# A state-space loop in another order: the turn-back split between two engines, input products dealt over three steps, half of a norm taken earlier

## The chip, the cores and the metric

The kernel runs on one core of a Trainium2 chip. The core has five engines that run on their own queues, each in order: TensorE (PE, matrix products into PSUM), VectorE (DVE, elementwise work and scans), ScalarE (ACT, functions and copies), GpSimd (POOL, here some elementwise work), SyncE (SP, here the queue that issues nearly all DMAs). They wait for each other through semaphores. The metric is the device time of the whole program in microseconds, the median of several runs. The profiled execution is one more run, with a trace of every instruction.

## The reference, cut to what matters

A trunk of two layers on one sequence of 512 positions and 1024 features. Each layer is a half-step SwiGLU, a token mixer and another half-step SwiGLU, all with an RMSNorm before and after. The mixer of layer 0 is an S5 state-space layer, that of layer 1 a convolution module. The change lies in layer 0:

```python
x = x + 0.5 * rmsnorm(swiglu(rmsnorm(x, g_pre)), g_post)
h = rmsnorm(x, norm_pre)
u = h @ w_in                               # 64 groups of 16
bu = einsum(u, B_bar)                      # complex, 64 states a group
st[t] = a_bar * st[t-1] + bu[t]            # complex scan over the positions
y = gelu(Re(C st) + d_skip * u)
z = y * sigmoid(y @ w_glu + b_glu)
h = z @ w_out
x = x + rmsnorm(h, norm_post)
```

All products are in float32. The kernel makes them of float32r halves: a matrix is split into a high part (rounded) and a low part (the rest), and three matmuls, high x high, high x low and low x high, make one product.

## The kernel before, in words

The six sub-layers run one after another (L1378): ffn, s5, ffn, ffn, conv, ffn. x stays in SBUF, features on the partitions, as eight pieces of 128 x 512. Weights come as units of 128 x 1024: `want(n)` (L87) splits unit n on ACT (L94, high part) and DVE (L98, low part) and issues the load (L83, on SP) of the unit three further on. `mm3` (L108) issues the three matmuls (L110 to L112). Buffers are pools whose tiles are handed out in program order: 39 pages of 128 x 1024, five `tmp`, eight PSUM banks, two `acc` and two `y` tiles. There is no planner here: the instructions stand on each engine in the order in which the Python code issues them.

**The seam.** `proj` (L251) ends a sub-layer. Its tail (L366) goes over 16 pieces (half A of the positions for k = 0 to 7, then half B) in steps s: `scaled` (DVE L350), `added` (DVE L354; ACT L173 makes the high half of the next input, L177 the square), `split_lo` (DVE L186, of the piece two steps back), `x_plus` (DVE L182, which adds the squares into acc2), and `entry_step`, 12 matmuls that start the next sub-layer's first four units with that piece. A small list `side` puts the three DVE steps of half B's output norm between them, one a step. The sum over features of acc2 is `stat`, a matmul with ones (L117); `rsqrt_steps` (L120) is one ACT function (L123) and three DVE operations (L125 to L127). Before, `entry_norm` (L241) takes this entry norm over all 512 positions at once, on PE after the first product of the next sub-layer.

**The state-space layer.** `s5` (L833) has eight units j of w_in. `win(j)` is unit j's product, 24 matmuls; 0 to 3 are done in the seam. `stack(j)` scales the bank with the norm (DVE L855), and a DMA writes it to DRAM; `unstack(j)` reads it back in another layout. Then nine steps s of a loop (L980) work on tile s of eight, several stages at once:

- `inputs(s)`: PE, 8 products (L867) into two banks (real and imaginary).
- `turn(s)`: four DVE products of banks with tables (L880, L881, L883, L884), a POOL sum (L882) and a DVE difference (L885).
- `scan(s)`: two DVE scans (L892), with coefficients made by `decay` (ACT L873, POOL L874).
- `back(s-1)`, the turn-back of the scanned tile: POOL memsets (L904), a POOL product (L905) and three DVE products (L906 to L908).
- `outputs(s-1)`: PE, 20 products (L917, L920) into a bank; `gelu(s-1)` on ACT (L925); `y_out`, `y_in`: a DMA to DRAM and, a step later, back in the old layout.
- `parts(s-3)`: the high and low halves of y, on ACT (L940) and DVE (L941).
- `glu_step(s-3)`: PE, 12 matmuls of the gate product with piece s-3, which need both halves.

The order inside a step is partly written out (inputs, for s = 0 and 1 a whole win(6 + s), back, the DMAs) and partly given by the string `S5_ORDER` (L25), one letter for each part: k stack, t turn, w want, p parts, d decay, o outputs, c scan, g glu_step, l gelu. So PE has inputs(s), outputs(s-1), glu_step(s-3) in that order, and DVE has back(s-1), stack, turn(s), the weight split, parts(s-3), scan(s).

Of the kernel before, what the change touches and what calls it, by code (L numbers as in the profile page):

```python
# [9 lines left out]
AF = mybir.ActivationFunctionType  # L10
# [3 lines left out]
NK = 8  # L14
# [7 lines left out]

C_TAPS = (31, 31, None, None, None, None, None, 23)
NL = 2
S5_ORDER = "ktwpdocgl"  # L25
S5_WANT = (8, 9, 10, 11, 11, 11, 11, 11, 11)
BUD_D = (3, 8, 18, 18, 18, 18)
FFN_AHEAD = 4
# [7 lines left out]
def trunk(ctx: ExitStack, tc: tile.TileContext, h, plan):  # L36
# [15 lines left out]
    def page(dt=F32R):  # L52
        return pages.tile([P, 2, T], dt, tag="pg", name=nm("pg"))
# [7 lines left out]
    def psum():  # L61
        return psp.tile([P, T], F32, tag="ps", name=nm("ps"))
# [24 lines left out]
    def want(n):  # L87
        while ptr["split"] <= min(n, NU - 1):
            u = ptr["split"]
            w_dma(u)  # L90
            r = raws.pop(u)
            hi, lo = page(), page()
            hv, lv = hi.rearrange("p a b -> p (a b)"), lo.rearrange("p a b -> p (a b)")
            ACT.copy(hv, r)  # L94
            if lo_engine[0] is None:
                late.append((lv, r, hv))
            else:
                lo_engine[0].tensor_tensor(lv, r, hv.bitcast(F32), op=ALU.subtract)  # L98
            halves[u] = tuple(v.rearrange("p (k m) -> p k m", m=P) for v in (hv, lv))
            ptr["split"] += 1  # L100
            w_dma(u + 3)
# [28 lines left out]
    def rsqrt(ps, y):  # L130
        for f in rsqrt_steps(ps, y):
            f()
# [4 lines left out]
    def y_tile():  # L137
        return statp.tile([P, T], F32, tag="y", name=nm("y"))
# [51 lines left out]
    def entry_step(k, cs, xn, u0, ps4, outs=range(4)):  # L190
        for j in outs:
            mm3(ps4[j][:, cs], u0 + j, k, xn[k][:, 0, cs], xn[k][:, 1, cs], k == 0, k == NK - 1)
# [55 lines left out]
            e["acc"] = stat_tile()  # L248
            DVE.tensor_scalar(e["acc"], ps, EPS_SUM, EPS_SUM / P, op0=ALU.add, op1=ALU.mult)

    def proj(u0, nk, rhs, post, nl, pre, xn, bias=None, lead=None, carried=None, defer=True):  # L251

        acc = stat_tile() if carried is None else carried
        acc2 = stat_tile()
# [106 lines left out]
            else:  # L361
                (nc.sync, nc.scalar)[k % 2].dma_start(out=h["out"][:, k, cs], in_=x[:, k, cs])

        side, sqs = [], {}
        at = (2, 5, 5, 6) if pre is None else (4, 4, 4, 5)
        for s in range(len(todo) + 2):  # L366
            if s < len(todo):
                if s == NK:
                    while side:
                        side.pop(0)()  # L370
                scaled(*todo[s])
            if side:
                side.pop(0)()
            if 1 <= s <= len(todo):
                added(*todo[s - 1])
            if pre is not None and s == at[0]:
                sq = square(NK - 1, pb, B)
            if s == at[1]:
                plus(sq, B)
                if pre is None:  # L380
                    copy(NK - 1, pb, B)
            if pre is not None and s == at[2]:
                sb = stat(acc[:, B])
            if pre is not None and s == at[3]:
                copy(NK - 1, pb, B)
            if s >= 2 and pre is not None:
                cs, k = todo[s - 2]
                split_lo(k, cs, xn, pre)
                if s == 2:
                    want_late()  # L390
                if not defer:
                    x_plus(sqs.pop((cs.start, k)), cs, acc2)
                entry_step(k, cs, xn, un, ps4)
            if pre is None and s == at[0]:
                sq = square(NK - 1, pb, B)
            if pre is None and s == at[2]:
                sb = stat(acc[:, B])
            if s == at[3]:
                side = rsqrt_steps(sb, y[:, B], carried is None)
        if pre is not None and defer:  # L400
            want(un + 4)
            for k in range(NK):
                x_plus(x_square(k, FULL, acc2), FULL, acc2)
        return {"xn": xn, "ps": ps4, "acc2": acc2, "u": un} if pre is not None else None

    def ffn(e, post, pre, defer=True):
        u0, xn = e["u"], e["xn"]
        g = []

        def evac(m, pa, pb):  # L410
            a = tmp()
            DVE.tensor_tensor(a, pa, e["y"], op=ALU.mult)  # L412
            ACT.activation(a, a, AF.Silu)  # L413
            DVE.tensor_tensor(a, pb, a, op=ALU.mult)  # L414
            t = page()
            ACT.copy(t[:, 0, :], a)  # L416
            DVE.tensor_tensor(t[:, 1, :], a, t[:, 0, :].bitcast(F32), op=ALU.subtract)  # L417
            g.append(t)

        pend = None  # L420
        want(u0 + 6)
        for m in range(2, NF):
            pa, pb = psum(), psum()
            for j, ps in enumerate((pa, pb)):
                want(u0 + 2 * m + j)
                for k in range(NK):
                    mm3(ps, u0 + 2 * m + j, k, xn[k][:, 0, :], xn[k][:, 1, :], k == 0, k == NK - 1)
                    if m == 2 and j == 0 and k == 4:
                        entry_norm(e, True)
                    if k == 3:  # L430
                        n = 2 * m - 4 + j
                        tick("D", PREP_FIRST[n] if n < len(PREP_FIRST) else PREP_UP)
            if FFN_AHEAD and m > 2:
                want(u0 + 2 * m + FFN_AHEAD)
            if m == 2:
                ACT.preload_act_table(AF.Silu)
                evac(0, e["ps"][0], e["ps"][1])
                evac(1, e["ps"][2], e["ps"][3])
            else:
                evac(*pend)  # L440
            pend = m, pa, pb
            want(u0 + 2 * m + 2)
        evac(*pend)
        return proj(u0 + 2 * NF, NF, g, post, 1, pre, g[:NK], carried=e["acc"], defer=defer)

# [385 lines left out]
    def s5(e, post, pre):  # L833
# [62 lines left out]
        def back(i):  # L896


            X, Y = wk.pop(i)
            c, s = (tabs[i][2][:, r, :, :n] for r in range(2))  # L900
            S = page(F32).rearrange("p r (q c) -> p r q c", q=4)
            st[i] = S, X
            for v in (S, X):
                POOL.memset(v[:, :, :, 0:1], 0.0)  # L904
            POOL.tensor_tensor(S[:, 0, :, 1:], Y[:, 0, :, :n], c, op=M)  # L905
            DVE.scalar_tensor_tensor(X[:, 0, :, 1:], Y[:, 1, :, :n], -1.0, s, op0=M, op1=M)  # L906
            DVE.tensor_tensor(S[:, 1, :, 1:], Y[:, 0, :, :n], s, op=M)  # L907
            DVE.tensor_tensor(X[:, 1, :, 1:], Y[:, 1, :, :n], c, op=M)  # L908
# [32 lines left out]
                DVE.tensor_tensor(t[:, 1, :], yf[i], t[:, 0, :].bitcast(F32), op=D)  # L941

        banks = {j: e["ps"][j] for j in range(4)}
        cf = {}

        def win(j, norm=False):
            want(u0 + j)
            banks[j] = psum()
            for k in range(NK):
                mm3(banks[j], u0 + j, k, xn[k][:, 0, :], xn[k][:, 1, :], k == 0, k == NK - 1)  # L950
                if norm and k == 0:
                    entry_norm(e)

        g0 = u0 + 8

# [8 lines left out]
        load(0, (0, 3, 2))  # L964
        load(1, (0, 3, 2))
        load(0, (1,))
        want(u0 + 5)
        win(4, True)
        ACT.preload_act_table(AF.Gelu_apprx_tanh)
        stack(0)  # L970
        stack(1)
        unstack(0)
        unstack(1)
        win(5)
        stack(2)
        decay(0)
        want(u0 + 6)
        load(2, (3,))
        g4, h4 = [], []
        for s in range(9):  # L980
            if s <= 7:
                inputs(s)
            if s <= 1:
                win(6 + s)
            if s == 3:
                g4.extend(psum() for _ in range(4))
            if s:
                back(s - 1)

            y_out(s - 2)  # L990
            load(s + 2, (0,))
            unstack(s + 2)
            load(s + 2, (2,))
            load(s + 1, (1,))
            y_in(s - 2)
            load(s + 3, (3,))
            wu = u0 + S5_WANT[s]
            for c in S5_ORDER:
                if c == "t" and s <= 7:
                    turn(s)  # L1000
                if c == "p":
                    parts(s - 3)
                if c == "k":
                    stack(s + 3)
                if c == "w":
                    want(wu)
                if c == "d":
                    decay(s + 1)
                if c == "c" and s <= 7:
                    scan(s)  # L1010
                if c == "g":
                    glu_step(0, g4, s - 3)
                if c == "o" and s:
                    po = outputs(s - 1)
                if c == "l" and s:
                    gelu(s - 1, po)
# [361 lines left out]
    for i, (kind, idx) in enumerate(subs):  # L1378
        pre = subs[i + 1][1] * 8 if i + 1 < len(subs) else None
        post = 48 + idx * 8  # L1380
        if kind == "ffn":
            e = ffn(e, post, pre, i + 1 == len(subs) or subs[i + 1][0] == "ffn")
        elif kind == "s5":
            e = s5(e, post, pre)
        else:
            e = conv(e, post, pre)
# [101 lines left out]
```

## Time and profile before

| | us |
|---|---|
| median of 3 runs (1899.56 to 1903.05) | 1901.44 |
| the profiled execution | 1902.18 |
| its span in the trace | 1900.3 |
| PE busy | 1867.7 (98%) |
| DVE busy | 1087.1 (57%) |
| ACT busy | 637.1 (34%) |
| POOL busy | 44.2 (2%) |
| mean granted PE clock | 0.995 |

Times inside the trace count from the start of the span. A row of a timeline has the start, the duration, the engine, the line of the kernel, the operation, the tiles (out<-in), shapes and a count; where a wait stood ahead of it, the idle time and what ended it stand in brackets. Consecutive DVE operations overlap a little in the records, so costs are best read from start to start. A row of a table of stretches has the stretch, its length, each engine's busy time and instruction count, the granted PE clock, the DMA engines' share and GB/s. Stage by stage: the first ffn ends at about 384, its seam runs to 416, the state-space loop from 427 to about 511, the rest of the layer to 590.

### The profile page before, as it was taken

How to read it: one execution, taken by the hardware profiler on the slowest of the kernel's cores; microseconds unless marked ns; L12 is line 12 of the kernel's file. 1: busy time of each engine (PE TensorE's matmuls, PEld its weight loads, DVE VectorE, ACT ScalarE, POOL GpSimd, SP SyncE). 2: the span in 40 equal slices, each digit the busy share in tenths (PEclk: the TensorE clock that was granted, in tenths of full speed). 3: DMA queues.
4: the chain of work that ended last, by engine and by line, in shares of the span. 5: the costliest groups of instructions: out<-in, count | busy, mean ns of one | idle time of the engine just before them, and what ended most of it. 6: DMA issues, size and time to landing. Idle time of an engine off the chain costs nothing.

```text
span 1900.3 us, 24034 instructions
## 1 busy us (share of the span) xinstructions
PE 1867.7 (98%) x9502; PEld 1590.8 (84%) x9502; DVE 1087.1 (57%) x1894; ACT 637.1 (34%) x920; POOL 44.2 (2%) x63
## 2 busy tenths in 40 slices
PE   9999999999999999999999999999999999999997
PEld 7788888898889888888898888889887988888886
DVE  7787566789858634332485433226976785433324
ACT  4323445251245422221343222214313653222211
POOL 2000000002200000000000000000000000000000
PEclk9999999999999999999999999999999999999998
DMA  4334448849422422322223322222572224232221
GB/s 162 111 125 159 149 118 235 281 165 339 158 71 89 145 89 95 101 81 90 100 78 122 108 92 89 89 89 78 207 263 79 78 67 133 94 106 82 96 89 45
DMA packets 101280, 235.06 MB, mean 124 GB/s; under 512 B 26160, under 2 KB 44080, under 8 KB 101168
## 3 DMA queue, kind: packets, MB, share of 16 engines
q1 hardware_dynamic: 99872, 232.46, 37.5%
q8 instruction: 74, 1.21, 0.3%
q10 hardware_dynamic: 1296, 1.07, 0.2%
q14 instruction: 38, 0.31, 0.0%
HBM read 209.77 MB, written 23.72 MB: 123 GB/s over the span
## 4 chain that ended last, share of the span: by engine, by line
PE 85%; DVE 8%; DMA 4%; issue 1%; ACT 1%; SPq 1%; DVEq 0%; ACTq 0%
PE ps L112 27%; PE ps L111 27%; PE ps L110 27%; PE ps L1203 2%; DMA pg<-f_d 1%; DVE pg L98 1%; DMA pg<-s5b 1%; DVE pg L892 1%; DVE pg L907 1%; PE ps L1170 1%; DVE x L354 1%; DVE tmp L350 1%; PE ps L741 1%; DVE pg L186 1%; PE ps L117 1%
## 5 line engine op out<-in xcount | busy, mean ns | idle before, releaser
L110 PE MATMUL ps<-pg,pg 128*128 128x512 f32 (+1 forms) x2808 | 1034.7, 368 | 6.3 <-ACT pg L1337 4.7
L111 PE MATMUL ps<-pg,pg 128*128 128x512 f32 (+1 forms) x2808 | 1029.7, 367 | 4.3 <-DVE pg L186 3.7
L112 PE MATMUL ps<-pg,pg 128*128 128x512 f32 (+1 forms) x2808 | 1027.8, 366 | 1.9 <-DVE pg L98 1.1
L111 PEld LDWEIGHTS ps<-pg,pg 128*128 128x128 f32 x2808 | 530.5, 189 | 95.8 <-DVE pg L186 8.5
L110 PEld LDWEIGHTS ps<-pg,pg 128*128 128x128 f32 x2808 | 530.6, 189 | 94.0 <-ACT pg L1337 5.1
L112 PEld LDWEIGHTS ps<-pg,pg 128*128 128x128 f32 x2808 | 530.4, 189 | 89.1 <-DVE pg L98 2.4
L98 DVE TENSOR_TENSOR pg<-raw,pg 128x1024 fp32r<-128x1024 f32 x305 | 362.1, 1224 | 111.0 <-ACT pg L94 75.7
L94 ACT CAST pg<-raw 128x1024 fp32r<-128x1024 f32 x310 | 311.2, 1047 | 109.0 <-PE ps L111 28.0
L414 DVE TENSOR_TENSOR tmp<-ps,tmp 128x512 f32<-128x512 f32 x88 | 60.9, 692 | 248.7 <-PE ps L112 219.6
L276 DVE TENSOR_TENSOR acc<-acc,tmp 128x512 f32<-128x512 f32 (+1 forms) x54 | 33.0, 611 | 249.0 <-ACT tmp L271 248.9
L413 ACT ACTIVATE tmp<-tmp 128x512 f32<-128x512 f32 x88 | 55.6, 632 | 281.7 <-DVE tmp L412 281.7
L416 ACT CAST pg<-tmp 128x512 fp32r<-128x512 f32 x88 | 54.6, 621 | 252.3 <-DVE tmp L414 250.5
L271 ACT ACTIVATE tmp<-ps 128x512 f32<-128x512 f32 (+1 forms) x45 | 24.3, 540 | 281.6 <-PE ps L112 281.2
L417 DVE TENSOR_TENSOR pg<-tmp,pg 128x512 fp32r<-128x512 f32 x88 | 61.0, 693 | 61.7 <-ACT pg L416 61.7
L412 DVE TENSOR_TENSOR tmp<-ps,y 128x512 f32<-128x512 f32 x88 | 60.5, 687 | 27.1 <-PE ps L112 27.1
L173 ACT ACTIVATE pg<-x,gsc 128x256 fp32r<-128x256 f32 x80 | 40.8, 510 | 67.4 <-DVE x L354 67.4
L1117 DVE SCALAR_TENSOR_TENSOR pg<-pg,vec,pg 128x512 f32<-128x512 f32 x79 | 52.9, 742 | 0.0
L186 DVE SCALAR_TENSOR_TENSOR pg<-x,gsc,pg 128x256 fp32r<-128x256 f32 (+1 forms) x88 | 48.4, 551 | 3.4 <-ACT pg L214 2.9
L354 DVE SCALAR_TENSOR_TENSOR x<-tmp,gsc,x 128x256 f32<-128x256 f32 x96 | 45.9, 479 | 0.0
L1203 PEld LDWEIGHTS ps<-pg,pg 128*128 128x128 f32 x360 | 41.0, 192 | 0.4
L1203 PE MATMUL ps<-pg,pg 128*128 128x128 f32 x360 | 41.0, 275 | 0.0
L920 PE MATMUL ps<-pg,pg 128*128 128x128 f32 x256 | 36.6, 285 | 4.5 <-POOL pg L905 4.0
(153 smaller groups left out, 841.3 us busy)
## 6 DMA issues: line engine op xcount, KB each, us to landing
raw<-w SPq DMA_DIRECT2D x262, 512.0 KB, 4.1
pg<-tab_d SPq DMA_DIRECT2D x24, 512.0 KB, 6.0
pg<-toep SPq DMA_DIRECT2D x20, 512.0 KB, 5.4
tab_d<-pg SPq DMA_DIRECT2D x16, 512.0 KB, 3.1
raw<-cv_w_in SPq DMA_DIRECT2D x16, 512.0 KB, 5.0
pg<-s5b SPq DMA_DIRECT2D x8, 512.0 KB, 7.9
pg<-f_d SPq DMA_DIRECT2D x32, 128.0 KB, 7.4
raw<-s_w_in SPq DMA_DIRECT2D x8, 512.0 KB, 4.5
```

What stands on the lines that cost most here:

```text
L94: ACT.copy(hv, r)
L98: lo_engine[0].tensor_tensor(lv, r, hv.bitcast(F32), op=ALU.subtract)
L110: PE.matmul(out, lhsT=hi[:, s, :], rhs=xh, start=start, stop=False)
L111: PE.matmul(out, lhsT=hi[:, s, :], rhs=xl, start=False, stop=False)
L112: PE.matmul(out, lhsT=lo[:, s, :], rhs=xh, start=False, stop=stop)
L186: DVE.scalar_tensor_tensor(xn[k][:, 1, cs], x[:, k, cs], g, xn[k][:, 0, cs].bitcast(F32), op0=ALU.mult, op1=ALU.subtract)
L354: DVE.scalar_tensor_tensor(x[:, k, cs], t[:, cs], gsc[:, post + k : post + k + 1], x[:, k, cs], op0=ALU.mult, op1=ALU.add)
L412: DVE.tensor_tensor(a, pa, e["y"], op=ALU.mult)
L413: ACT.activation(a, a, AF.Silu)
L414: DVE.tensor_tensor(a, pb, a, op=ALU.mult)
L417: DVE.tensor_tensor(t[:, 1, :], a, t[:, 0, :].bitcast(F32), op=ALU.subtract)
L1203: PE.matmul(ps[:, q * P : q * P + P], lhsT=op[ND * q + d], rhs=z[:, q, 8 - d : 8 - d + P], start=d == 0, stop=d == ND - 1,)
```

## The change

Four things are changed.

1. `back` is cut in two. `back(s-1)` keeps the memsets and POOL's product (L905); the three DVE products become `back_rest(s-1)`. The order string gets a and b for them and becomes `aktbwpdcgol`: POOL's product (a), stack (k), turn (t), the three DVE products (b), want, parts, decay, scan (c), glu_step (g), outputs (o), gelu. With this `back` moves behind the DMAs of the step, and glu_step ahead of outputs.
2. The products of w_in's units 5, 6 and 7 are dealt out: three of unit 5's eight pieces ahead of inputs(0), the rest and unit 6 in step 0, unit 7 in halves in steps 1 and 2.
3. In the seam ahead of the state-space layer the entry norm of half A is taken at step 12: `stat` on PE and L123 on ACT, and its three DVE steps go into the steps after it (list `more`). Half B is left to `entry_rest`, ahead of win(4).
4. The split of unit 5 (`want(u0 + 5)`) now comes after the first two `stack` and `unstack`, and the load of ACT's Gelu table after it.

```diff
-S5_ORDER = "ktwpdocgl"
+S5_ORDER = "aktbwpdcgol"
...
+    def entry_rest(e):
+        rsqrt(stat(e["acc2"][:, HALVES[1]]), e["y"][:, HALVES[1]])
...
-        side, sqs = [], {}
+        side, sqs, more = [], {}, []
+        ye = None
...
             if side:
                 side.pop(0)()
+            elif more:
+                more.pop(0)()
...
                 entry_step(k, cs, xn, un, ps4)
+                if early and s == NK + 4:
+                    ye = y_tile()
+                    more = rsqrt_steps(stat(acc2[:, A]), ye[:, A])
...
             X, Y = wk.pop(i)
             c, s = (tabs[i][2][:, r, :, :n] for r in range(2))
+            turned[i] = X, Y, c, s
...
             POOL.tensor_tensor(S[:, 0, :, 1:], Y[:, 0, :, :n], c, op=M)
+
+        def back_rest(i):
+            S = st[i][0]
+            X, Y, c, s = turned.pop(i)
             DVE.scalar_tensor_tensor(X[:, 0, :, 1:], Y[:, 1, :, :n], -1.0, s, op0=M, op1=M)
             DVE.tensor_tensor(S[:, 1, :, 1:], Y[:, 0, :, :n], s, op=M)
             DVE.tensor_tensor(X[:, 1, :, 1:], Y[:, 1, :, :n], c, op=M)
...
-        def win(j, norm=False):
-            want(u0 + j)
-            banks[j] = psum()
-            for k in range(NK):
+        def win(j, ks=range(NK)):
+            if ks[0] == 0:
+                want(u0 + j)
+                banks[j] = psum()
+            for k in ks:
                 mm3(banks[j], u0 + j, k, xn[k][:, 0, :], xn[k][:, 1, :], k == 0, k == NK - 1)
-                if norm and k == 0:
-                    entry_norm(e)
...
-        want(u0 + 5)
-        win(4, True)
-        ACT.preload_act_table(AF.Gelu_apprx_tanh)
+        want(u0 + 4)
+        entry_rest(e)
         stack(0)
         stack(1)
         unstack(0)
         unstack(1)
-        win(5)
+        want(u0 + 5)
+        ACT.preload_act_table(AF.Gelu_apprx_tanh)
+        win(4)
         stack(2)
         decay(0)
+        win(5, range(3))
+        inputs(0)
         want(u0 + 6)
         load(2, (3,))
...
-            if s <= 7:
+            if 1 <= s <= 7:
                 inputs(s)
-            if s <= 1:
-                win(6 + s)
+            if s == 0:
+                win(5, range(3, NK))
+                win(6)
+            if s == 1:
+                win(7, range(4))
+            if s == 2:
+                win(7, range(4, NK))
...
-            if s:
-                back(s - 1)
...
             for c in S5_ORDER:
+                if c == "a" and s:
+                    back(s - 1)
+                if c == "b" and s:
+                    back_rest(s - 1)
```

`ffn` and `proj` get an argument `early`, true for the ffn ahead of the state-space layer, and `proj` hands `ye` on as the entry's y.

More of the change, by code (lines that the diff above doesn't have):

```diff
@@ L249, in entry_norm, with proj @@
             DVE.tensor_scalar(e["acc"], ps, EPS_SUM, EPS_SUM / P, op0=ALU.add, op1=ALU.mult)
-    def proj(u0, nk, rhs, post, nl, pre, xn, bias=None, lead=None, carried=None, defer=True):
+    def entry_rest(e):
+        rsqrt(stat(e["acc2"][:, HALVES[1]]), e["y"][:, HALVES[1]])
+    def proj(u0, nk, rhs, post, nl, pre, xn, bias=None, lead=None, carried=None, defer=True, early=False):
         acc = stat_tile() if carried is None else carried
@@ L403, in proj, with ffn @@
                 x_plus(x_square(k, FULL, acc2), FULL, acc2)
-        return {"xn": xn, "ps": ps4, "acc2": acc2, "u": un} if pre is not None else None
-    def ffn(e, post, pre, defer=True):
+        return {"xn": xn, "ps": ps4, "acc2": acc2, "u": un, "y": ye} if pre is not None else None
+    def ffn(e, post, pre, defer=True, early=False):
         u0, xn = e["u"], e["xn"]
@@ L443, in ffn @@
         evac(*pend)
-        return proj(u0 + 2 * NF, NF, g, post, 1, pre, g[:NK], carried=e["acc"], defer=defer)
+        return proj(u0 + 2 * NF, NF, g, post, 1, pre, g[:NK], carried=e["acc"], defer=defer, early=early)
     if any(k == "s5" for k, _ in plan["subs"]):
@@ L943, in s5 @@
         banks = {j: e["ps"][j] for j in range(4)}
-        cf = {}
-        def win(j, norm=False):
-            want(u0 + j)
-            banks[j] = psum()
-            for k in range(NK):
+        cf, turned = {}, {}
+        def win(j, ks=range(NK)):
[3 more added lines that the diff above has]
+            for k in ks:
                 mm3(banks[j], u0 + j, k, xn[k][:, 0, :], xn[k][:, 1, :], k == 0, k == NK - 1)
-                if norm and k == 0:
-                    entry_norm(e)
         g0 = u0 + 8
@@ L1381, in trunk @@
         if kind == "ffn":
-            e = ffn(e, post, pre, i + 1 == len(subs) or subs[i + 1][0] == "ffn")
+            after = subs[i + 1][0] if i + 1 < len(subs) else "ffn"
+            e = ffn(e, post, pre, after == "ffn", after == "s5")
         elif kind == "s5":
```

## The prediction

> **What bounds the kernel now.** I read the page first, then busy time by stretch, then the timelines of the engines inside the state-space loop (step s is one turn of the loop at L980). The page says that TensorE (PE) sets the time almost everywhere.
>
> ```profile
> span 1900.3 us, 24034 instructions
> PE 85%; DVE 8%; DMA 4%; issue 1%; ACT 1%; SPq 1%; DVEq 0%; ACTq 0%
> ```
>
> The change touches the loop and the seam ahead of it. So I cut the loop at the PE starts of `inputs(s)` (L867), s = 0 to 7, and at the end of `glu_step(6)`.
>
> ```profile
> core 0: us, PE busy (x) PEld busy (x) DVE busy (x) ACT busy (x) POOL busy (x), PEclk, DMA share, GB/s
> 427.35:434.59 7.24, 7.24 (x41) 6.29 (x40) 5.91 (x8) 1.06 (x1) 1.38 (x3) 1.00 0.99 338
> ...
> 453.41:467.91 14.50, 11.29 (x71) 10.37 (x70) 14.40 (x17) 4.21 (x7) 3.39 (x7) 0.88 1.03 358
> 467.91:477.49 9.58, 9.33 (x70) 8.55 (x69) 9.51 (x13) 1.85 (x4) 3.11 (x6) 1.00 1.00 344
> 486.53:495.52 8.99, 8.99 (x69) 8.51 (x68) 8.92 (x12) 1.30 (x3) 3.11 (x6) 1.00 0.32 109
> 495.52:504.51 8.99, 8.99 (x70) 8.51 (x69) 8.92 (x12) 1.11 (x2) 3.08 (x5) 1.00 0.18 60
> 504.51:516.05 11.54, 10.50 (x65) 9.15 (x64) 6.82 (x8) 3.95 (x5) 1.25 (x1) 1.00 0.21 64
> ```
>
> From 477 on, PE and VectorE (DVE) are both full, 8.99 us a step: a gain on DVE alone is worth nothing there. Only step 3 (14.50 us) has a large hole on PE, 3.2 us.
>
> One full step on DVE, and the GpSimd (POOL) product beside it:
>
> ```profile
> 486.04 0.69 DVE L906 SCALAR_TENSOR_TENSOR pg<-pg,pg 128x508 f32<-128x508 f32 x1
> 486.64 1.75 DVE L907 TENSOR_TENSOR pg<-pg,pg 128x508 f32<-128x508 f32 x1
> 488.31 0.68 DVE L908 TENSOR_TENSOR pg<-pg,pg 128x508 f32<-128x508 f32 x1
> 488.91 0.68 DVE L880 TENSOR_TENSOR pg<-ps,pg 128x512 f32<-128x512 f32 x1
> 489.51 0.68 DVE L881 TENSOR_TENSOR pg<-ps,pg 128x512 f32<-128x512 f32 x1
> ...
> 491.42 0.69 DVE L885 TENSOR_TENSOR pg<-pg,pg 128x512 f32<-128x512 f32 x1
> 492.03 0.68 DVE L941 TENSOR_TENSOR pg<-pg,pg 128x512 fp32r<-128x512 f32 x1
> 492.63 2.33 DVE L892 TENSOR_TENSOR_SCAN pg<-acc,pg 128x512 f32<-128x512 f32 x2
> ...
> 486.18 1.67 POOL L905 TENSOR_TENSOR pg<-pg,pg 128x508 f32<-128x508 f32 x1
> ```
>
> And the same step on PE: inputs 488.31 - 486.53 = 1.78 us, outputs 492.70 - 488.31 = 4.39, the gate product 495.52 - 492.70 = 2.82.
>
> ```profile
> 486.53 1.95 PE L867 MATMUL ps<-pg,pg 128*128 128x128 f32 x16
> 488.31 0.39 PE L917 MATMUL ps<-pg 128*128 128x128 f32 x2
> 492.70 0.48 PE L110 MATMUL ps<-pg,pg 128*128 128x512 f32 x1
> 495.52 0.72 PE L867 MATMUL ps<-pg,pg 128*128 128x128 f32 x5
> ```
>
> L907 takes 1.75 us beside POOL's L905 where its twin L908 takes 0.68: it stands until POOL is done. That loss of 1.07 us a step is what moving POOL's product beside the bank operations removes.
>
> **The order, followed through.** The new order string decides more than that product. Before, DVE did the turn-back of s-1, then the turn of s, then `parts(s-3)` (L941); PE did inputs(s), outputs(s-1), gate product(s-3). Now DVE does turn(s) first, then the three turn-back products, then L941, then the scan; and PE does inputs(s), gate product(s-3), outputs(s-1). The gate product needs L941 of the same step:
>
> ```profile
> 474.10 0.69 DVE L941 TENSOR_TENSOR pg<-pg,pg 128x512 fp32r<-128x512 f32 x1
> ...
> 474.85 0.49 PE L111 MATMUL ps<-pg,pg 128*128 128x512 f32 x1 [0.25 <-DVE pg L941]
> ```
>
> So L941 to PE costs 0.75 us, and before, L941 was just in time with 4.39 us of outputs ahead of it on PE. Now nothing of PE stands between inputs and that wait, and L941 itself is queued on DVE behind a turn that cannot start until PE's inputs are through. It becomes one chain per step: inputs, turn, turn-back, L941, gate product, outputs, next inputs. Queued on PE behind the waiting gate product are outputs(s-1) and inputs(s+1), and DVE's next turn waits for those.
>
> How soon DVE follows inputs shows where it waited for them, in step 0:
>
> ```profile
> 427.35 1.95 PE L867 MATMUL ps<-pg,pg 128*128 128x128 f32 x16
> ...
> 428.44 0.69 DVE L880 TENSOR_TENSOR pg<-ps,pg 128x512 f32<-128x512 f32 x1 [4.55 <-PE ps L867]
> 429.33 0.69 DVE L881 TENSOR_TENSOR pg<-ps,pg 128x512 f32<-128x512 f32 x1 [0.20 <-PE ps L867]
> ...
> 436.57 0.69 DVE L906 SCALAR_TENSOR_TENSOR pg<-pg,pg 128x508 f32<-128x508 f32 x1
> ```
>
> With S the PE start of inputs: L881 starts at S + 1.98 (429.33 - 427.35); L885 1.91 later (489.51 to 491.42), S + 3.89; L906 0.61 later, S + 4.50; L907, no longer held, at 5.10; L908 at 5.70; L941 at 6.31; PE goes on at 7.06. Then eleven twelfths of the gate product, 2.59, and outputs, 4.39: **the next inputs at S + 14.04**, against 8.99. In steps 1 and 2 there is no gate product. Outputs wait only for L908: S + 5.70 + 0.75, then 32 of their 40 instructions, 4.39 x 0.8 = 3.51: S + 9.96. POOL's product falls into the time in which DVE waits for inputs, so its own length alone (between L907's surplus of 1.07 and L905's 1.67) costs nothing; should it still hold L907, the chain is 1.07 longer.
>
> **The seam.** Half of the entry's norm is done inside the seam: a sum over half A on PE after the entry product of s = 12, then ScalarE (ACT), then three DVE operations, one each at s = 13, 14, 15. Rows of a like group, the DVE split of s = 12, the first PE product of s = 17 and the first after the seam (1.44 us for 12 products), the old `stack(0)`, and a weight load:
>
> ```profile
> 383.54 0.67 PE L117 MATMUL ps<-acc,ones 128*128 128x256 f32 x2 [0.33 <-DVE acc L276]
> 384.25 0.38 ACT L123 ACTIVATE tmp<-ps 128x256 f32<-128x256 f32 x1 [1.31 <-PE ps L117]
> 406.11 0.47 DVE L186 SCALAR_TENSOR_TENSOR pg<-x,gsc,pg 128x256 fp32r<-128x256 f32 x1
> 414.11 0.28 PE L110 MATMUL ps<-pg,pg 128*128 128x256 f32 x1
> 415.55 0.40 PE L110 MATMUL ps<-pg,pg 128*128 128x512 f32 x1
> 420.27 1.89 DVE L855 TENSOR_TENSOR tmp<-ps,y 128x512 f32<-128x512 f32 x3
> ...
> raw<-s_w_glu SPq DMA_DIRECT2D x8, 512.0 KB, 5.1
> ```
>
> At s = 13 the first of the three stands in DVE's queue at about 407.2. The sum on PE comes only after the 12 entry products of s = 12 (from 414.11 - 5 x 1.44 = 406.9 to 408.3); by 384.25 - 383.54 = 0.71 and ACT's 0.38 DVE can go on at 409.5. DVE stands 2.3 us; behind it wait the adds and splits that feed PE's entry products, so PE's seam ends about 3.0 us later (0.65 of it the sum itself). After the seam PE runs half B's sum (0.65 in place of the whole's 0.87) and 33 matmuls of 0.23 us, 7.6, to inputs(0) at about 426.9; `stack(0)` comes about 0.9 us later than 420.27, at 421.1, and inputs(0) need its round trip through DRAM, which took at most 427.35 - 420.27 = 7.1 us: 428.2 at the latest. Before, PE came to inputs(0) without a wait, so I take PE's own arrival, S0 = 426.9, a gain of 0.4 us. Bounds: 424.5 if DVE does not stand (gain 2.9), 428.2 if the trip takes all of 7.1 (loss 0.9).
>
> Moved past queues: `want(u0+5)` now comes behind `stack` and `unstack`, so one weight load on SP's queue waits behind two round trips, until about 425; with 5.1 us to land it is there at 430, and its split on DVE is due after turn(0), past 432. Cover 2 us, cost nothing. win(7) dealt over steps 1 and 2 puts 2.8 us of PE work ahead of outputs in each, inside DVE's chain there, and holds the eight pages of its input a step longer; the loads behind them are due two steps on.
>
> **The sum.** PE from S0: inputs 1.78, then 15 matmuls of win(5) (3.45) and win(6) (5.53): S1 = 437.6. S2 = 447.6, S3 = 457.6. Step 3 also has a weight split ahead of L941:
>
> ```profile
> L98 DVE TENSOR_TENSOR pg<-raw,pg 128x1024 fp32r<-128x1024 f32 x5 | 6.0, 1214 | 0.0
> ...
> 509.74 1.06 PE L920 MATMUL ps<-pg,pg 128*128 128x128 f32 x8
> 511.97 0.69 DVE L941 TENSOR_TENSOR pg<-pg,pg 128x512 fp32r<-128x512 f32 x1 [4.46 <-ACT pg L940]
> ```
>
> S4 = 457.6 + 14.04 + 1.2 = 472.8, and four steps of 14.04 bring S8 = 529.0. In step 8 the gate product (2.82) and outputs (4.39) do not wait: 536.2. Next is gate product 6. Its L941 follows outputs(7) by 511.97 - 510.6 = 1.4 us (outputs end 0.89 after the row at 509.74) and PE by 0.75 more; before, gate product 5 covered this, now it costs 1.9: 536.2 + 1.9 + 2.82 = 540.9 against 516.05. **The loop loses 24.9 us**, the saved 8 x 1.07 on DVE included, which lie in its waits.
>
> **The clock.** PE would stand some 5.0 us (S + 2.0 to 7.06) in each of steps 3 to 7. What such a hole does to the granted clock shows once:
>
> ```profile
> 458.69 1.90 PE L920 MATMUL ps<-pg,pg 128*128 128x128 f32 x8 [3.10 <-POOL pg L905]
> ...
> 458.69:463.30 4.61, 4.50 (x22) 4.29 (x23) 4.58 (x8) 0.00 (x0) 1.36 (x3) 0.63 1.02 375
> ```
>
> A mean of 0.63 over 4.61 us is 3.41 us at half speed, at most 1.7 us lost. For a hole of 5.0 us, part of the slow stretch falls into the hole; I take 1.4 each, between 0 and 2.1: 5 x 1.4 = 7 (0 to 11). The Trainium skill (TensorE: Matmul & The Clock Gate, Part 1: The HAM clock gate) would grant half speed only after a whole idle window of about 3.4 us; here 3.10 was enough, so the trace decides. By the page a 5.0 us hole holds a whole window in about half of the phases, and 7 would be some 4, an estimate.
>
> **Total**: 24.9 + 7 = 32 on the profiled execution's own 1902.18 us (span 1900.3 and 1.9 around it), 1934; that execution is 0.7 above the median 1901.44, so **1933 us**. With the bounds of seam and clock 1924 to 1940.
>
> **Rivals.**
> (a) *The gate product does not wait for L941* (its low half ready early). Then every step is 9.96: S8 = 457.6 + 5 x 9.96 = 507.4, plus 2.82 + 4.39 + 1.9 + 2.82 = 519.3, 3.3 us over 516.05: 1905. For it: the high half needs only ACT. Against: the row at 474.85 waits for L941, and the string puts p behind t and b.
> (b) *Faster: PE paces every step.* If DVE runs ahead so far that neither the turn-back nor L941 is waited for, PE from S0 has win work 14.5, eight inputs 14.2, eight outputs 35.1 and seven gate products 19.7 = 83.5, ending at 510.4, 5.7 us early: 1896. The hole of step 3 filled with half of win(7) speaks for it; it decides as soon as L941 is done 2 us after S. Against: turn(s) needs the inputs of its own step, 1.98 us after S, and five operations follow.
> (c) *The clock stays low through two stretches each time*: 5 x 3.4 = 17, 1943.
> (d) *The change doesn't free L907*: 1.07 on each chained step, 1938.
>
> **Chances.** Forecast 0.75 (its own range 1924 to 1942), (a) 0.08, (b) 0.06, (c) 0.06, (d) 0.02, no change by parts that cancel 0.03. Range 1918 to 1945, which leaves out (a), (b), no change and a little above. Within 0.2% (3.8 us) is what a measurement of this kernel can't tell from none: faster 0.06, same 0.03, slower 0.91.
>
> **What would show it.** In the changed trace: L907 near 0.68 us, L905 beside stack or in DVE's wait; PE waiting about 5 us at L111 for L941 in steps 3 to 7, L880 waiting for L867; 14 us or more between L867 groups from step 3 on; granted clock under 1 in those steps; one DVE wait of about 2 us at the seam's first half-norm operation. I am wrong if L867 groups stay 9 to 10 us apart, or if PE's matmuls don't wait for L941.

## The result, and the profile after

The changed kernel takes 1943.03 us, the median of four runs (1940.85 to 1943.52), against 1901.47 before (1899.56 to 1903.05). The ratio is 1.0213, with a 95% interval of 1.0201 to 1.0225. Its profiled execution took 1943.52 us with a span of 1941.7; the span grew by 41.4.

Lines have moved: inputs are L877 (L867 before), the turn is L890 to L895 (L880 to L885), POOL's product L916 (L905), the three DVE products of the turn-back L921 to L923 (L906 to L908), the scan L902 (L892), outputs L932 and L935 (L917 and L920), the GELU L940 (L925), y's halves L955 on ACT and L956 on DVE (L940 and L941).

First the busy time by stretch of the changed kernel, cut at the same places as before: the start of `inputs(s)` for s = 0 and 3 to 7, the end of step 7 on PE (there the last work is now `outputs(6)`, before it was `glu_step(4)`), the end of `glu_step(6)`.

```profile
core 0: us, PE busy (x) PEld busy (x) DVE busy (x) ACT busy (x) POOL busy (x), PEclk, DMA share, GB/s
...
382.00:428.83 46.83, 43.85 (x313) 40.27 (x311) 39.10 (x89) 24.01 (x47) 0.10 (x1) 1.00 0.43 149
428.83:459.86 31.03, 30.29 (x192) 26.64 (x193) 26.33 (x34) 5.27 (x7) 6.81 (x13) 1.00 0.97 342
459.86:477.92 18.06, 12.32 (x70) 10.76 (x69) 9.86 (x14) 2.56 (x4) 4.00 (x7) 0.81 0.67 233
477.92:494.92 17.00, 12.13 (x70) 10.76 (x69) 7.92 (x11) 1.62 (x3) 2.68 (x5) 0.80 0.52 170
494.92:511.95 17.03, 12.16 (x70) 10.79 (x69) 7.92 (x11) 1.62 (x3) 2.68 (x5) 0.80 0.40 140
511.95:527.40 15.45, 10.58 (x70) 9.47 (x69) 7.92 (x11) 1.62 (x3) 2.68 (x5) 0.89 0.22 69
527.40:543.60 16.20, 11.34 (x70) 9.98 (x68) 10.87 (x14) 1.10 (x2) 3.05 (x4) 0.79 0.10 32
543.60:557.50 13.90, 11.07 (x67) 9.15 (x66) 3.83 (x5) 5.05 (x7) 0.00 (x0) 1.00 0.19 62
557.50:631.00 73.50, 72.19 (x369) 61.33 (x368) 41.32 (x62) 31.86 (x45) 0.00 (x0) 1.00 0.35 112
```

And of the kernel before, the stretches that the prediction did not show:

```profile
382.00:427.35 45.35, 44.38 (x308) 40.73 (x307) 36.50 (x84) 23.73 (x47) 0.10 (x1) 1.00 0.48 165
427.35:453.41 26.06, 25.82 (x177) 23.52 (x176) 24.60 (x31) 3.72 (x5) 7.60 (x13) 1.00 0.95 330
...
516.05:589.50 73.45, 72.17 (x369) 61.26 (x368) 40.47 (x62) 31.74 (x45) 0.00 (x0) 1.00 0.33 110
```

| stretch | before | after | more |
|---|---|---|---|
| to inputs(0), from 382 | 45.35 | 46.83 | 1.5 |
| inputs(0) to inputs(3) | 26.06 | 31.03 | 5.0 |
| inputs(3) to the end of step 7 | 51.10 | 83.74 | 32.6 |
| from there to the end of glu_step(6) | 11.54 | 13.90 | 2.4 |
| the rest of the layer | 73.45 | 73.50 | 0.0 |

The sum is 41.5 of the 41.4 us. Most of it, 32.6, lies in steps 3 to 7, in which PE does inputs, gate product and outputs, each 15 to 18 us long where the last ones before were 8.99, at a granted clock of 0.8 to 0.9.

One of these steps on DVE, on PE and on POOL, each from the timeline of the changed kernel:

```profile
479.02 0.69 DVE L890 TENSOR_TENSOR pg<-ps,pg 128x512 f32<-128x512 f32 x1 [8.20 <-PE ps L877]
479.91 0.69 DVE L891 TENSOR_TENSOR pg<-ps,pg 128x512 f32<-128x512 f32 x1 [0.20 <-PE ps L877]
...
481.83 0.69 DVE L895 TENSOR_TENSOR pg<-pg,pg 128x512 f32<-128x512 f32 x1
482.44 0.68 DVE L921 SCALAR_TENSOR_TENSOR pg<-pg,pg 128x508 f32<-128x508 f32 x1
483.04 0.68 DVE L922 TENSOR_TENSOR pg<-pg,pg 128x508 f32<-128x508 f32 x1
483.63 0.68 DVE L923 TENSOR_TENSOR pg<-pg,pg 128x508 f32<-128x508 f32 x1
484.23 0.69 DVE L956 TENSOR_TENSOR pg<-pg,pg 128x512 fp32r<-128x512 f32 x1
484.83 2.33 DVE L902 TENSOR_TENSOR_SCAN pg<-acc,pg 128x512 f32<-128x512 f32 x2
496.02 0.69 DVE L890 TENSOR_TENSOR pg<-ps,pg 128x512 f32<-128x512 f32 x1 [8.85 <-PE ps L877]
```

```profile
477.92 1.95 PE L877 MATMUL ps<-pg,pg 128*128 128x128 f32 x16
479.63 0.47 PE L110 MATMUL ps<-pg,pg 128*128 128x512 f32 x1
484.97 0.80 PE L111 MATMUL ps<-pg,pg 128*128 128x512 f32 x1 [4.87 <-DVE pg L956]
...
489.83 0.63 PE L932 MATMUL ps<-pg 128*128 128x128 f32 x2
...
494.92 1.95 PE L877 MATMUL ps<-pg,pg 128*128 128x128 f32 x16
```

```profile
487.34 1.27 POOL L916 TENSOR_TENSOR pg<-pg,pg 128x508 f32<-128x508 f32 x1
```

The turn-back product that had stood beside POOL's (L907 before, L922 now) is down from 1.75 to 0.68 us, as the change has it. But DVE waits 8 us for inputs, and PE 4.87 us for L956. The waits of the stretch 425 to 560, in total, times and longest:

```profile
PE ps L111 <- DVE pg L956: 25.3, 7, 5.4
...
DVE pg L890 <- PE ps L877: 39.0, 8, 8.9
```

### The profile page after: what moved, and what is told of

It is laid out like the page before. It is cut to its first block, busy times and chain, and to the rows that moved or that the text cites. A ratio compares the mean times of both kernels' runs of the same rounds, so it can differ in the third digit from the quotient of the medians.

```text
span 1941.7 us, 24032 instructions
## 1 busy us (share of the span) xinstructions
PE 1883.1 (97%) x9504; PEld 1600.8 (82%) x9504; DVE 1081.2 (56%) x1897; ACT 637.0 (33%) x921; POOL 41.3 (2%) x63
## 4 chain that ended last, share of the span: by engine, by line
PE 92%; DVE 5%; DMA 1%; issue 1%; ACT 1%; SPq 0%; DVEq 0%; ACTq 0%
PE ps L111 28%; PE ps L112 28%; PE ps L110 28%; PE ps L1227 2%; PE ps L935 1%; PE ps L751 1%; DVE x L358 1%; PE ps L1194 1%; PE ps L877 1%; DVE tmp L354 1%; DVE pg L186 1%; PE ps L117 1%; PE ps L1152 0%; PE ps L932 0%; DMA u_d<-tmp 0%
## 5 line engine op out<-in xcount | busy, mean ns | idle before, releaser
L94 ACT CAST pg<-raw 128x1024 fp32r<-128x1024 f32 x310 | 311.5, 1047 | 107.3 <-PE ps L111 28.1
L1227 PE MATMUL ps<-pg,pg 128*128 128x128 f32 x360 | 41.0, 275 | 0.0
L354 DVE TENSOR_TENSOR tmp<-pg,y 128x256 f32<-128x256 f32 x96 | 39.7, 419 | 0.5
```

Of the source, the lines that this page charges most:

```text
L354: DVE.tensor_tensor(t[:, cs], hs[k][:, cs], y[:, cs], op=ALU.mult)
L1227: PE.matmul(ps[:, q * P : q * P + P], lhsT=op[ND * q + d], rhs=z[:, q, 8 - d : 8 - d + P], start=d == 0, stop=d == ND - 1,)
```

## The experiments

Theory: the new order makes one chain of each step (inputs, turn, turn-back, L956, gate product, outputs, next inputs), 14.0 us long, and the holes that it leaves on PE cost a half clock on top. The rivals: the gate product's place alone, the turn's place alone, the dealt products, the norm in the seam, or slow matmuls that hide in waits.

### The order alone

Added to the kernel before: `back_rest` and the new string.

```diff
-S5_ORDER = "ktwpdocgl"
+S5_ORDER = "aktbwpdcgol"
...
-            if s:
-                back(s - 1)
```

> The kernel before with the split of the turn-back and the new order string alone: input products and entry norm as before. Chain theory: the loss is all in the order, 1936 to 1941 us (some 4 us less than the changed kernel, whose inputs(3) come later). Rival (the dealt input products or the norm in the seam make a good part of the loss): under 1930 us.

Measured: 1940.90 us, 1.0208 of before (1.0178 to 1.0237). From inputs(3) on its steps are 16.6 to 17.3 us apart. So the order makes the loss; the other parts of the change account for some 2 us of it, which the overlapping intervals leave open.

### The holes filled

```diff
                 if c == "g":
+                    if 3 <= s <= 7:
+                        ex = psum()
+                        for i in range(24 if s == 3 else 20):
+                            PE.matmul(ex[:, :P], lhsT=ones, rhs=ones, start=True, stop=True)
                     glu_step(0, g4, s - 3)
```

> The changed kernel with 20 extra products of ones (24 in step 3) on PE between inputs and the gate product in steps 3 to 7, which fill most of each hole and whose result is overwritten by nothing that is used; this adds work and changes no result. If the half clock after each hole costs what the trace says (12 us over five steps): granted clock 1.0, 14.0 us a step, 1929 to 1933 us. Rival (the slow stretches hide in waits for DVE): 1940 us or more.

Measured: 1929.56 us, 13.5 less than the changed kernel, with some 100 more matmuls in it. The busy time of its steps 3 to 6:

```profile
457.45:472.73 15.28, 14.63 (x118) 13.86 (x117) 9.87 (x14) 2.56 (x4) 4.02 (x7) 1.00 0.79 267
472.73:486.85 14.12, 13.72 (x111) 12.98 (x110) 7.92 (x11) 1.62 (x3) 2.68 (x5) 1.00 0.64 205
486.85:500.99 14.14, 13.74 (x111) 12.97 (x110) 7.92 (x11) 1.62 (x3) 2.68 (x5) 1.00 0.50 168
500.99:515.13 14.14, 13.74 (x111) 12.97 (x110) 7.92 (x11) 1.62 (x3) 2.69 (x5) 1.00 0.25 75
```

Granted clock 1.00, and 14.12 to 14.14 us a step (15.28 in step 3): the chain without the clock, beside the 14.04 and 15.2 worked out. The half clock does not hide in the waits: it is 12 to 13.5 of the 41 us.

### Outputs ahead of the gate product

```diff
-S5_ORDER = "aktbwpdcgol"
+S5_ORDER = "aktbwpdcogl"
```

> The changed kernel with outputs ahead of the gate product on PE again, all else as changed (the turn still ahead of the turn-back on DVE). Chain theory: outputs now wait for L923 (turn-back), at 6.45 us after the inputs' start, run to 9.96, and the gate product to 12.8, with L941's work covered: 12.8 us a step and a PE hole of 3.7 us, with 0 to 1.8 us lost to the half clock in each; 1918 to 1932 us, 1928 the likeliest. Rival (the gate product's place alone makes the loss): about 1903 us.

Measured: 1925.62 us, ratio 1.0127 (1.0098 to 1.0157). Steps are 13.8 to 14.5 us: the 12.8 of the chain and 1.0 to 1.7 for the clock, which falls for 3.41 us in steps 3 to 6 and for 6.83 in step 7. PE waits no longer for L956 but for the turn-back (waits from 420 to 640):

```profile
PE ps L935 <- DVE pg L921: 14.5, 6, 2.9
```

So the gate product's place makes less than half of the loss, 17 us. With outputs first again, the turn ahead of the turn-back still costs 24 us; how much it costs depends on what PE has to do meanwhile, as the next two runs show.

### The halves of y first

```diff
-S5_ORDER = "aktbwpdcgol"
+S5_ORDER = "apwktbdcgol"
```

> The changed kernel with the halves of y (parts) and the weight split put ahead of the turn on DVE, so that the gate product finds its low half ready; turn still ahead of turn-back, gate product ahead of outputs. Chain theory: 9.96 us a step, PE holes under 1 us, granted clock 1.0 in steps 3 to 7, 1904 to 1912 us. Rival (turn ahead of turn-back alone makes the loss): steps stay at 14 us or more, over 1930 us.

Measured: 1922.37 us, ratio 1.0110 (1.0081 to 1.0139). The expectation missed: steps 1 to 3 take 13.1 to 13.9 us, step 4 takes 11.3 and the next 10.7. Of the steps, the clock fell in 1, 2 and 3 alone. DVE's waits from 425 to 530, and, from the timelines of ACT and DVE, one of them:

```profile
DVE pg L956 <- ACT pg L955: 19.4, 6, 4.2
DVE pg L98 <- ACT pg L94: 10.2, 3, 5.4
```

```profile
490.63 0.60 ACT L940 ACTIVATE tmp<-ps 128x512 f32<-128x512 f32 x1 [9.65 <-PE ps L935]
491.12 0.61 ACT L955 CAST pg<-pg 128x512 fp32r<-128x512 f32 x1
...
491.76 0.69 DVE L956 TENSOR_TENSOR pg<-pg,pg 128x512 fp32r<-128x512 f32 x1 [2.81 <-ACT pg L955]
```

ACT's queue is in order: the GELU (L940) waits for outputs, and behind it stand the cast of y (L955) and of the weights (L94), for which DVE now waits ahead of the turn. I had followed DVE's and PE's queues and left ACT's out.

### The same, with ACT's part made earlier

```diff
-S5_ORDER = "aktbwpdcgol"
+S5_ORDER = "apktbwdcgohl"
...
+                if c == "h":
+                    parts_hi(s - 2)
```

(`parts_hi` is the ACT half of `parts`; the DVE half is now L962. "e2" is the run just above.)

> e2 missed: with parts and the weight split ahead of the turn, DVE waited for ACT, whose copy of y's high half and weight casts stand behind the GELU of the outputs just made. Here ACT makes the high half a step earlier, ahead of the GELU, DVE's low half (L962) stands ahead of the turn, and the weight split stays behind the turn-back. So neither is waited for, and what is left of the chain is inputs, turn, turn-back, outputs: 9.96 us a step from step 4 on (some 13 in step 3, where the last weight split is due), granted clock 1.0: 1905 to 1911 us. Rival (another wait takes the place again): 10.6 us a step or more, over 1915 us.

Measured: 1909.64 us, ratio 1.0039 (1.0025 to 1.0053). Steps 4 to 6 take 10.13 us each, beside the 9.96 expected. Step 3 takes 15.7, more than the 13 expected; the waits of PE from 420 to 560 name the late weight split, and the clock fell for 6.83 us after it:

```profile
PE ps L112 <- DVE pg L98: 4.2, 2, 4.0
...
PE ps L935 <- DVE pg L921: 0.2, 1, 0.2
```

With L956 out of the way 33 us of the loss are gone, but the shorter chain, 10.1 us, is still longer than the 8.99 of before. What remains is the turn ahead of the turn-back. This is rival (a) made; it was put at 1905.

### The old order with the other two parts

```diff
-S5_ORDER = "aktbwpdcgol"
+S5_ORDER = "abktwpdocgl"
```

> The changed kernel with the old order of parts (turn-back whole and ahead of the turn, outputs ahead of the gate product); dealt input products and the half norm in the seam stay. Chain theory: no chain, DVE paces steps 1 to 4 and PE the rest as before, and what is left is the shift of inputs(0), -1 to +2 us: 1899 to 1903 us. Rival (the dealt products delay the later inputs for good): 1905 us or more.

Measured: 1901.81 us, ratio 1.0001 (0.9992 to 1.0010). This run is called e3 below. Without the new order nothing is lost and nothing won.

### One part at a time on the kernel before

The input products dealt out alone (win(5) in two pieces around inputs(0), win(7) in two halves):

> The kernel before with the input products of units 5 to 7 dealt over steps 0 to 2 and nothing else. inputs(0) is then bound by its DRAM round trip, some 1.3 us earlier, and DVE paces the loop from there; the hole in step 3 fills with work that only moves: 1899 to 1901 us. Rival (the filled hole is worth its 3 us and its half clock): 1895 to 1897 us.

Measured: 1901.30 us, ratio 0.9997 (0.9988 to 1.0006), the same as before. Step 3's hole of 3.10 us is down to one of 1.38 (the step takes 11.31 us in place of 14.50), but the idle time has only moved: now PE waits for the DRAM round trip ahead of inputs(0), and a stretch of half clock, 3.41 us, follows it. PE's waits from 400 to 560:

```profile
PE ps L867 <- DMA pg<-u_d: 2.0, 1, 2.0
```

The half norm alone (with its rest ahead of win(4) and the later split):

> The kernel before with the half norm in the seam, its rest ahead of win(4) and the later split of unit 5, and nothing else. DVE stands 2.3 us at the first of the three steps, PE's seam ends 3 us later and inputs(0), still behind the whole of win(5), some 4.7 us later: 1904 to 1907 us. Rival (the seam's delay is hidden): 1901 us.

Measured: 1904.23 us, ratio 1.0014 (1.0005 to 1.0022), at the edge of the expectation. Inputs(0) starts 2.7 us later than before, not the 4.7 expected. So the half norm in the seam costs 2.5 us by itself; with the dealt products, which put 15 matmuls behind inputs(0), it is made good (e3, 1901.8).

### The stand in the seam taken away

```diff
-            elif more:
+            elif more and s >= NK + 7:
```

with the old order, as in the run above that has the old order and the other two parts.

> As e3, and the three DVE steps of the half norm start at seam step 15 in place of 13, so that DVE doesn't stand for the sum. The stand of 2.3 us measured at L125 should go, inputs(0) come some 2.4 us earlier and all that DVE paces with it: 2 to 3 us under e3, 1898 to 1900 us. Rival (the stand is hidden anyway): the same as e3.

Measured: 1899.35 us, ratio 0.9991 (0.9982 to 0.9999), 2.5 us under the old order with the early steps. The stand is real and costs about what it lasts, 2.3 us. This run is e8 in the next expectation.

### POOL's product on DVE

In the kernel before, and then in the last variant:

```diff
-            POOL.tensor_tensor(S[:, 0, :, 1:], Y[:, 0, :, :n], c, op=M)
+            DVE.tensor_tensor(S[:, 0, :, 1:], Y[:, 0, :, :n], c, op=M)
```

> The kernel before with POOL's turn-back product on DVE and nothing else changed. L907 should fall from 1.75 to 0.68 us; the gain of 0.47 us counts only in steps 1 to 4 that DVE paces: 1.5 to 2.5 us less than before, 1899 to 1900 us. If the gain reached every step, 3.8 us.

> As e8, and POOL's turn-back product is done by DVE, so that nothing holds L922: one product of 0.60 more and a stand of 1.07 less, 0.47 us off each step that DVE paces (1 to 4): 1.9 us under e8, 1895 to 1898 us.

Measured: in the kernel before 1897.63 us, ratio 0.9982 (0.9973 to 0.9991); in the variant 1895.76 us, ratio 0.9971 (0.9961 to 0.9982). The first gains twice what was expected. Its trace gives 2.5 us between inputs(0) and inputs(7), as expected, and 1.6 in the last step, where outputs(7) had waited 0.93 us for POOL's product, which I had left out; the rest there is the shorter turn-back itself. DVE in the kernel before with this edit, one turn-back:

```profile
490.75 0.66 DVE L905 TENSOR_TENSOR pg<-pg,pg 128x508 f32<-128x508 f32 x1
491.33 0.68 DVE L906 SCALAR_TENSOR_TENSOR pg<-pg,pg 128x508 f32<-128x508 f32 x1
491.93 0.68 DVE L907 TENSOR_TENSOR pg<-pg,pg 128x508 f32<-128x508 f32 x1
492.53 0.68 DVE L908 TENSOR_TENSOR pg<-pg,pg 128x508 f32<-128x508 f32 x1
```

Four products take 2.4 us on DVE alone; the three with POOL's beside them took 2.9. And the steps 1 to 4 of the last variant, which is faster than both kernels:

```profile
434.81:443.79 8.98, 8.98 (x69) 8.50 (x68) 8.95 (x13) 0.00 (x0) 1.50 (x4) 1.00 1.04 396
443.79:452.78 8.99, 8.99 (x70) 8.51 (x69) 8.96 (x13) 2.05 (x3) 1.50 (x4) 1.00 1.01 328
452.78:462.87 10.09, 9.28 (x70) 8.51 (x69) 10.06 (x15) 3.27 (x5) 1.47 (x4) 1.00 1.01 341
462.87:471.89 9.02, 9.02 (x69) 8.55 (x68) 8.99 (x15) 1.74 (x3) 1.48 (x4) 1.00 1.02 370
```

PE has work in all of them but 0.8 us of step 3. The variant is 1.9 us under the one-line edit of the kernel before; their intervals overlap, but few of their single times do (1894.17 to 1897.22 against 1896.57 to 1899.76). With the product still on POOL the same two parts, without the stand, were 2.4 us under the kernel before. So in the old order the dealt products and the half norm together seem to win some 2 us; which of the two makes it is not shown.

## Why the prediction was right, and where its sizes were off

**The chain.** Right, part by part. L891 follows inputs by 479.91 - 477.92 = 1.99 (1.98 predicted), L895 by 3.91 (3.89), L923 by 5.71 (5.70), L956 by 6.31 (6.31), PE goes on at 7.05 (7.06). Steps 1 and 2 take 10.17 and 10.13 us (9.96). With the clock held up, a whole step takes 14.13 (14.04). The time itself, 1943, lies 10 us above the 1933 and just above the forecast's own range of 1924 to 1942; only the range drawn wider, to 1945, holds it.

**The clock.** This is the term that was mis-sized most: 1.4 us a hole, 7 in all, with a bound of 2.1 a hole, 11 in all. Measured are 12.4, above the bound: the five stretches' 83.74 less 15.2 and four times 14.04. I took one slow stretch of 3.41 us a hole, as in the trace of before. At four of the five holes the clock stayed low for two. In steps 3 to 5 they began only 0.6 to 0.8 us before PE went on, so that nearly all of them fell on work; in step 7 they began 2.4 us before, and the step lost 2.2. Those of step 4:

```profile
484.31:491.13 6.82, 6.16 (x18) 5.10 (x19) 2.86 (x4) 0.00 (x0) 1.32 (x2) 0.50 0.59 197
```

Of the 6.82 us PE worked 6.16 at half speed, some 3 us lost. Only the hole of step 6 had one stretch, and its step lost the 1.4 that I took for each. That is rival (c)'s mechanism, which I gave 0.06; its price of 3.4 for each of five holes was too high. That its 1943 is the measured time is partly chance, because other terms below make up the difference. The Trainium skill's rule (TensorE: Matmul & The Clock Gate, Part 1: The HAM clock gate), half speed after a whole idle window of about 3.4 us, would have given some 4 us in all, an estimate. The trace went against it again: all five holes brought the slow clock, and in other runs holes of 1.79 to 2.54 us did so too.

**The tail.** "In step 8 the gate product and outputs do not wait" was wrong. ACT's cast for gate product 5 stands behind the GELU of outputs(6), with no inputs ahead on PE to cover it:

```profile
544.96 0.51 PE L110 MATMUL ps<-pg,pg 128*128 128x512 f32 x1 [1.19 <-ACT pg L955]
```

So gate product 5 takes 4.71 us from the end of step 7, not 2.82. The same wait follows once more, ahead of gate product 6, as predicted. Together the tail is 13.9 us, 2.0 over the 11.9 of the sum.

**The seam.** DVE stood 2.29 us (2.3 predicted) at the first step of the half norm:

```profile
411.20 0.43 DVE L125 SCALAR_TENSOR_TENSOR tmp<-tmp 128x256 f32<-128x256 f32 x1 [2.29 <-ACT tmp L123]
```

Inputs(0) came 1.5 us later than before in place of 0.4 earlier. But the sum over half B of the output norm (L117), ahead of all that the change touches, already stands at 394.95 in place of 393.30: the seam's own part is 0.2 us earlier. That 1.65 us, from code that is the same in both, is a difference between executions: over the traces of the eleven other runs the same row stands at 391.02 to 394.69.

The sum again: 32 predicted, and 5.4 for the clock, 2.0 for the tail, 1.65 ahead of the seam and 0.3 in steps 0 to 2 make the 41.4.

**The rivals.** (a), no wait for L956, was made in the run that prepares y's halves early: 1909.6, and still slower than before, as its 9.96 us a step said (10.13 measured). (b), PE pacing every step, is not reached by this order at all, but the last variant comes near it: 1895.8, beside 1896. (d) did not happen where the turn stands between; in step 8, where it doesn't, L922 takes 1.76 us again.

## What to carry to other kernels

When the order of a loop is changed, write down for one step which instruction each engine's next one waits for, on all queues, ACT's too, and go round once: if the chain comes back to its start by way of another engine, its length is the step, however little each engine works. A saving on an engine that ends up waiting is worth nothing. Put between a producer and its consumer on another engine the work that needs neither, and look first for that cover when two parts change places.

## What the runs showed of the hardware that was not expected

The half clock comes after smaller holes on PE than the one of 3.10 us in the trace of before, and mostly lasts longer after larger ones. In the run with the halves of y first, holes of 1.79, 2.21 and 2.54 us were each followed by 3.41 us at half speed, those of 1.04 and 0.47 us by none; the wait of 2.0 us ahead of inputs(0) with the dealt products alone also brought 3.41. Four of the changed kernel's five holes, of 4.86 to 5.39 us, brought 6.83, one 3.41. The size alone does not decide: with outputs first, four holes of 2.85 or 2.86 us brought 3.41 and a fifth 6.83, and a hole of 1.76 us in the seam brought none in the changed kernel, but 3.41 in the run with the halves of y first (from 411.91, 1.4 us after the hole). Two steps of the changed kernel took 17.00 and 17.03 us, close to five times 3.41: slow stretches start 17.07 us apart there (467.24, 484.31, 501.37, 518.44).

POOL's product of 128 x 508 took 1.27 us while DVE read a bank or waited, 1.67 beside DVE's SBUF products, and 2.09 where a weight split ran beside its first half (440.15 in the run with the halves first). Giving it to DVE, at 0.6, was faster in both kernels in which it was tried.
